# Hybrid decoder trunk: the first layer's x, AV and CV columns packed per k tile, zero matmuls during the first loads, two load queues, and the rstd spread moved

## The chip, the core and the metric

The kernel runs on one core of a Trainium2 chip. The metric is the device time of one execution in microseconds (us), lower is better; a kernel's time is the median of several executions. TensorE (PE) multiplies, ScalarE (ACT) and VectorE (DVE) do the elementwise work, GpSimd (POOL) a little scalar work, and the sync engine (SP) issues nearly all loads.

## What is computed

Two layers over x of 256 rows (t) by 1024 columns; each projects one RMS-normalised x to 3584 columns, feeds three branches, gates them and adds an output projection to x. Cut to what matters here:

```python
hn = rms_norm(x, norm_gain)
proj = jnp.einsum('bsd,de->bse', hn, w_in)
a_q, a_k, a_v, a_g, b_x, b_g, c_q, c_k, c_v, c_g = jnp.split(proj, _in_split_points(), axis=-1)
y_a = dilated_attention(rope(a_q), rope(a_k), a_v) * jax.nn.silu(a_g)      # 8 heads of 64
y_b = rg_lru_branch(b_x, ...) * jax.nn.silu(b_g)
y_c = stick_breaking_attention(c_q, c_k, c_v) * jax.nn.silu(c_g)           # 4 heads of 64
x = x + jnp.einsum('bse,ed->bsd', jnp.concatenate([y_a, y_b, y_c], axis=-1), w_out)
```

All of it is float32. After the second layer a last rms_norm follows.

## The kernel before

**Split products.** Every projection is made of three float32r products: an operand is split into a high part (a rounded copy by ScalarE, L106 or L114) and a low part (the difference, by VectorE, L107 or L115), and hi*hi, hi*lo and lo*hi are summed in PSUM (`mm3`, L166 to L172). `xh`, `xl` hold x transposed, as eight k tiles of 128 by 256; `whi`, `wlo` a chunk of weights.

**Chunks.** The weights of a layer are 18 chunks of 128 by 2048 (1 MB): AV in two chunks (four k tiles of 512 columns each), CV, CQ, CK and the others (eight k tiles of 256 columns). `load_chunk` (L95) loads a chunk into two staging tiles `st` (five buffers) and splits it in pieces of 512 columns; `whi` and `wlo` have four buffers each. `weights(l, c)` (L120) has the chunks up to two ahead of c loaded and split. The tile framework puts the instructions of ScalarE, VectorE and the queues into an order of its own; TensorE's order is the program's.

**The start.** The first layer doesn't normalise x ahead of the projections: x is multiplied by the gain alone (`first_x`, L110, the gain is a 257th column of the x tile), and 1/rms (`rstd`) is multiplied into the projections' outputs. All loads are on SP: eight pairs of an x tile (128.5 KB) and a k tile of AV (256 KB) in turn, then CV, x itself (`xres`), constants, the small parameters `prm_t` and CQ. TensorE does AV per k tile for both t halves (L259 to L264, 48 matmuls of 512 columns), then CV (48 of 256).

**The rstd spread.** `rstd0` is computed by `rms_stats` from `xres` (L276). V of both branches gets it as a per-row scale (L286 to L289). The transposed outputs (q, k and so on) need it along the free axis: L278 to L282 put it on a diagonal, multiply that with ones on TensorE (`rb_ps`, two matmuls) and copy the result to `rb`. `scaled` (L291) multiplies an output with `rb`; `rp0` is the rope table times `rb` (L472).

**Next.** CQ and CK give qc and kc; the projection of AQ[0] follows, and between its two halves `sb_scores` (L333) multiplies kc with qc. `proj_b(c, mid)` makes a projection in two halves of 24 matmuls and calls `mid` between them.

Of the kernel before, what the change touches and what calls it, by code (L numbers as in the profile page):

```python
# [9 lines left out]
F32 = mybir.dt.float32  # L10
F32R = mybir.dt.float32r
# [4 lines left out]
P = 128  # L16
S = 256
# [26 lines left out]


@with_exitstack
def trunk_kernel(ctx: ExitStack, tc: tile.TileContext, x, xt, wpack, prm_d, gatew, gains, consts, rope, out):
    nc = tc.nc
    act, dve, pe, gps = nc.scalar, nc.vector, nc.tensor, nc.gpsimd

# [35 lines left out]
        return a.rearrange("p (b t) -> p b t", b=n)  # L86

    LN_EXP, SIGM = "natural_log_exp_and_others", "sigmoid_and_others"
    table(LN_EXP)
    ctx.enter_context(tc.manual_schedule(engines={mybir.EngineType.PE}))  # L90

    xh = sb.tile([P, NK, S], F32R, name="xh", tag="xh")
    xl = sb.tile([P, NK, S], F32R, name="xl", tag="xl")

    def load_chunk(l, c, parts=2, between=None):  # L95
        hi = wsp.tile([P, 2048], F32R, name="whi", tag="whi")
        lo = wsp.tile([P, 2048], F32R, name="wlo", tag="wlo")
        w = 2048 // parts
        for i in range(parts):
            if between:  # L100
                between(i)
            st = wst.tile([P, 1024], F32, name="st", tag="st")
            nc.sync.dma_start(out=st[:, 0:w], in_=wpack[l, c][:, i * w:(i + 1) * w])
            for j in range(0, w, 512):
                ws, ss = slice(i * w + j, i * w + j + 512), slice(j, j + 512)
                act.activation(hi[:, ws], st[:, ss], AF.Copy)  # L106
                dve.tensor_sub(lo[:, ws], st[:, ss], hi[:, ws].bitcast(F32))  # L107
        return hi, lo

    def first_x(k):  # L110
        xg = scr(S + 1)
        nc.sync.dma_start(out=xg, in_=xt[k])
        g = xg[:, S:S + 1]
        act.activation(xh[:, k, :], xg[:, 0:S], AF.Copy, scale=g)  # L114
        dve.scalar_tensor_tensor(xl[:, k, :], xg[:, 0:S], g, xh[:, k, :].bitcast(F32), ALU.mult, ALU.subtract)  # L115

    order = [(l, c) for l in range(L) for c in range(NCH)]
    ready = {}
    pending = list(order)

# [4 lines left out]
            ready[i] = load_chunk(*i)  # L125
        return ready.pop((l, c))

    for i in range(2):
        ready[pending.pop(0)] = load_chunk(0, CH_AV + i, 4, lambda j, i=i: first_x(4 * i + j))
    ready[pending.pop(0)] = load_chunk(0, CH_CV)  # L130

    xres = cst.tile([P, NT, D], F32, name="xres")
    for t in range(NT):
        nc.sync.dma_start(out=xres[:, t, :], in_=x[t * P:(t + 1) * P, :])
# [1 line left out]
    ident = con[:, C_ID:C_ID + P]  # L136
    nmask = con[:, C_NM:C_NM + 384]
    nc.sync.dma_start(out=con, in_=consts[:, 0:C_CM])
    prm_t = cst.tile([P, L, SM_P], F32, name="prm_t")
    nc.sync.dma_start(out=prm_t, in_=prm_d)  # L140
    ready[pending.pop(0)] = load_chunk(0, CH_CQ)

    tiny = cst.tile([P, 1], F32, name="tiny")
    dve.memset(tiny, 1e-19)
# [30 lines left out]
    nc8 = cst.tile([P, L * 2], F32, name="nc8")  # L175

    def log_sigmoid_lambda():
        lam = prm_t.rearrange("p l (b j) -> p (l b) j", b=2)[:, :, 7:8].rearrange("p b j -> p (b j)")

        def tn(name):  # L180
            return wk.tile([P, L * 2], F32, name=name, tag=name, bufs=1)

        lneg, labs, e, d2, sv, s2, acc, lmin = [tn(f"ls{i}") for i in range(8)]
        gps.tensor_scalar(lneg, lam, -1.0, None, ALU.mult)
        dve.tensor_tensor(labs, lam, lneg, ALU.max)
        tab(e, labs, AF.Exp, scale=-1.0)
# [18 lines left out]
    gn = cst.tile([P, D], F32, name="gn", tag="gn")  # L205

    for l in range(L):
        prm = prm_t[:, l, :].rearrange("p (b j) -> p b j", b=2)
        if l > 0:
            xh = sb.tile([P, NK, S], F32R, name="xh", tag="xh")  # L210
            xl = sb.tile([P, NK, S], F32R, name="xl", tag="xl")
# [20 lines left out]
        def rows(ps, b=2):  # L232
            return v2(ps, b), rb.rearrange("p (o t) -> p o t", o=1).broadcast_to([P, b, S])

        if l == 0:
            av_w = [weights(l, CH_AV + i, 0) for i in range(2)]
        else:
            for t in range(NT):
                rstd = rms_stats(t)
                for half in range(2):  # L240
                    xn = scr(512)
                    cs = slice(half * 512, half * 512 + 512)
                    dve.scalar_tensor_tensor(xn, xres[:, t, cs], rstd, gn[:, cs], ALU.mult, ALU.mult)
                    tp = bank(at, "s")
                    for j in range(4):
                        pe.transpose(tp[:, j * P:(j + 1) * P], xn[:, j * P:(j + 1) * P], ident)  # L246
                    ks = slice(half * 4, half * 4 + 4)
                    split_psum(tp.rearrange("p (k c) -> p k c", k=4),
                               xh[:, ks, t * P:(t + 1) * P], xl[:, ks, t * P:(t + 1) * P])
                if t == 0:  # L250
                    av_w = [weights(l, CH_AV + i) for i in range(2)]
                    av_ps = [bank(at, "s")]
                    for i in range(2):
                        proj_a(av_ps[0], av_w[i], 0, 4 * i, 4, 512, i == 0, i == 1)

        if l == 0:
            av_ps = [bank(at, "s") for _ in range(NT)]
            for i in range(2):
                for k in range(4):  # L259
                    for t in range(NT):  # L260
                        v = [a.rearrange("p (k c) -> p k c", c=512)[:, k:k + 1, :].rearrange("p k c -> p (k c)")
                             for a in av_w[i]]
                        proj_a(av_ps[t], v, t, 4 * i + k, 1, 512, i + k == 0, i + k == 4)
            cv_w = weights(l, CH_CV, 1)  # L264
        else:
# [340 lines left out]
    return wp  # L606


def _pack_small(conv_w, conv_b, gate_a_w, gate_a_b, gate_x_w, gate_x_b, lru_lambda):
    pr = np.zeros((P, L, SM_P), np.float32)  # L610
    gw = np.zeros((P, L, SM_W), np.float32)
    for l in range(L):
        for b in range(2):
            r = slice(b * P, b * P + P)
            o = 8 * b
            pr[:, l, o:o + 4] = conv_w[l][:, r].T
            pr[:, l, o + 4] = conv_b[l][r]
            pr[:, l, o + 5] = gate_a_b[l].reshape(-1)[r]
            pr[:, l, o + 6] = gate_x_b[l].reshape(-1)[r]
            pr[:, l, o + 7] = lru_lambda[l][r]  # L620
# [7 lines left out]
def _arrays(x, norm_gain, w_in, conv_w, conv_b, gate_a_w, gate_a_b, gate_x_w, gate_x_b,  # L628
# [32 lines left out]
```

## Time and profile before

| | |
|---|---|
| median of 3 runs | 258.06 us (257.77 to 258.25) |
| the profiled execution | 257.8 us, span 256.0 us |
| TensorE busy | 243.4 us, 95% of the span |
| VectorE, ScalarE busy | 191.5 us (75%), 166.2 us (65%) |
| mean granted TensorE clock | 0.994 |
| chain that ended last | PE 93%, ACT 3%, DMA 1% |
| DMA | 43.44 MB, mean 170 GB/s |

The span runs from the first to the last instruction; the execution's own time is 1.8 us longer. The busy share of an engine is an average over all stages. The chain is followed back from the last instruction, at each step to what released it. Idle time stands with what ended it.

### The profile page before, as it was taken

The page shows a single profiled execution, that of the slowest core. Times are in us where ns is not written, and L with a number is a line of the kernel's source. Part 1 is how long each engine was busy: PE and PEld are TensorE (multiplying, and loading weights), DVE is VectorE, ACT ScalarE, POOL GpSimd, SP SyncE. Part 2 cuts the span into 40 slices and gives each one's busy share as a digit, 9 for nine tenths or more (in the row PEclk, how much of TensorE's full clock was granted, in tenths as well). Part 3 has the DMA queues.
Part 4 walks back from the last instruction along what each step waited for, and adds up shares of the span by engine and source line. Part 5 has one row for each costly group of instructions (what it writes and reads, how often), then busy time and mean ns, then how long its engine had stood idle before and what let it go on. Part 6 is the DMA issues. An engine that isn't in the chain of part 4 may idle for free.

```text
span 256.0 us, 4715 instructions
## 1 busy us (share of the span) xinstructions
PE 243.4 (95%) x1764; PEld 222.7 (87%) x1764; DVE 191.5 (75%) x431; ACT 166.2 (65%) x359; POOL 8.2 (3%) x29
## 2 busy tenths in 40 slices
PE   1999999999999999999999999999999999999990
PEld 1789899999999989878877999999999998987870
DVE  3864797999999669988685634499999846985253
ACT  4859866964684875994664555594486496795143
POOL 0003800000000000000000000000000000000000
PEclk9999999999999999999999999999999999999997
DMA  6999889854336840258466667532644642000022
GB/s 167 342 353 414 308 232 332 280 188 135 113 111 223 278 159 15 67 186 263 143 195 215 209 208 226 183 87 79 177 155 121 236 139 82 3 0 0 3 82 82
DMA packets 14134, 43.44 MB, mean 170 GB/s; under 512 B 1696, under 2 KB 2848, under 8 KB 14112
## 3 DMA queue, kind: packets, MB, share of 16 engines
q1 hardware_dynamic: 14112, 43.15, 50.6%
q8 instruction: 14, 0.23, 0.4%
q14 instruction: 8, 0.07, 0.1%
HBM read 42.09 MB, written 1.05 MB: 169 GB/s over the span
## 4 chain that ended last, share of the span: by engine, by line
PE 93%; ACT 3%; DMA 1%; DVE 0%; issue 0%; SPq 0%
PE pp L172 67%; PE s L172 13%; PE y L328 3%; PE s L396 2%; PE s L418 2%; ACT whi L106 1%; PE s L369 1%; PE pp L444 1%; DMA st<-w_pack 1%; PE s L342 1%; ACT scr L154 1%; PE s L246 0%; PE s L349 0%; PE s L367 0%; PE s L345 0%; ACT vc L289 0%
## 5 line engine op out<-in xcount | busy, mean ns | idle before, releaser
L107 DVE TENSOR_TENSOR wlo<-st,whi 128x512 fp32r<-128x512 f32 x144 | 93.1, 686 | 24.0 <-ACT whi L106 22.7
L106 ACT ACTIVATE whi<-st 128x512 fp32r<-128x512 f32 x144 | 82.1, 624 | 30.8 <-PE pp L172 10.5
L172 PE MATMUL pp<-xh,whi 128*128 128x256 f32 x352 | 50.8, 286 | 0.5 <-ACT whi L106 0.5
L172 PE MATMUL pp<-xl,whi 128*128 128x256 f32 x352 | 49.4, 283 | 0.0
L172 PE MATMUL pp<-xh,wlo 128*128 128x256 f32 x352 | 49.4, 283 | 0.0
L172 PEld LDWEIGHTS pp<-xh,whi 128*128 128x128 f32 x352 | 45.9, 191 | 2.4 <-issue 1.3
L172 PEld LDWEIGHTS pp<-xh,wlo 128*128 128x128 f32 x352 | 45.4, 192 | 0.0
L172 PEld LDWEIGHTS pp<-xl,whi 128*128 128x128 f32 x352 | 45.4, 192 | 0.0
L81 ACT ACTIVATE pr<-scr,mn 128x128 f32<-128x128 f32 (+1 forms) x32 | 14.1, 441 | 9.9 <-DVE mn L404 9.9
L172 PE MATMUL s<-whi,xh 128*128 128x512 f32 x32 | 11.9, 432 | 5.6 <-ACT whi L106 5.3
L154 ACT ACTIVATE scr<-xres 128x512 f32<-128x512 f32 x12 | 7.5, 626 | 12.9 <-DVE xres L542 12.8
L172 PE MATMUL pp<-whi,yh 128*128 128x512 f32 x48 | 14.1, 394 | 0.0
L172 PE MATMUL pp<-wlo,yh 128*128 128x512 f32 x48 | 13.8, 390 | 0.0
L172 PE MATMUL pp<-whi,yl 128*128 128x512 f32 x48 | 13.8, 389 | 0.0
L316 ACT ACTIVATE yh<-scr 128x512 fp32r<-128x512 f32 x8 | 5.0, 630 | 12.7 <-DVE scr L315 12.7
L172 PEld LDWEIGHTS s<-whi,xh 128*128 128x128 f32 x32 | 6.4, 205 | 7.4 <-ACT whi L106 5.3
L75 ACT ACT_TABLE_LOAD x9 | 11.5, 1283 | 0.9 <-PEq L654 0.7
L172 PE MATMUL s<-wlo,xh 128*128 128x512 f32 x32 | 11.6, 424 | 0.0
L81 ACT ACTIVATE scr<-scr 128x384 f32<-128x384 f32 (+1 forms) x20 | 10.8, 542 | 0.8 <-DVE scr L294 0.5
L172 PE MATMUL s<-whi,xl 128*128 128x512 f32 x32 | 11.3, 413 | 0.0
L172 PEld LDWEIGHTS pp<-wlo,yh 128*128 128x128 f32 x48 | 9.0, 188 | 1.9
L172 PEld LDWEIGHTS pp<-whi,yl 128*128 128x128 f32 x48 | 9.0, 188 | 1.9
(139 smaller groups left out, 321.6 us busy)
## 6 DMA issues: line engine op xcount, KB each, us to landing
st<-w_pack SPq DMA_DIRECT2D x68, 512.0 KB, 5.0
st<-w_pack SPq DMA_DIRECT2D x8, 256.0 KB, 4.6
scr<-x_t SPq DMA_DIRECT2D x8, 128.5 KB, 4.4
xres<-x_in SPq DMA_DIRECT2D x2, 512.0 KB, 7.8
out<-scr SPq DMA_DIRECT2D x4, 256.0 KB, 2.2
gw_t<-gate_w SPq DMA_DIRECT2D x2, 256.0 KB, 6.1
gn<-gains SPq DMA_DIRECT2D x1, 512.0 KB, 7.2
gf<-gains SPq DMA_DIRECT2D x1, 512.0 KB, 4.5
```

Of the source, the lines that this page charges most:

```text
L75: load = act.preload_act_table_set(name)
L81: i = dep(act.activation(*a, **k), loaded["load"])
L106: act.activation(hi[:, ws], st[:, ss], AF.Copy)
L107: dve.tensor_sub(lo[:, ws], st[:, ss], hi[:, ws].bitcast(F32))
L154: act.activation(scr(512), xres[:, t, i * 512:(i + 1) * 512], AF.Square, accum_out=sq[:, i:i + 1])
L172: pe.matmul(ps, a(k), b(k), start=first and i == 0, stop=last and i == len(seq) - 1)
L316: act.activation(yh[:, k0:k0 + n, :], dst, AF.Copy)
L328: pe.matmul(y[hr, p * 128 + o:p * 128 + 256], vt[:, s0, hs], wts[i][:, ws], start=s0 == 0, stop=s0 == 1)
L342: pe.matmul(zs[h][:, 0:256], kc[hr, hb, 0:128], qc[hr, hb, :], start=True, stop=True)
L369: pe.matmul(z[:, 0:384], trir[:, 0, :], sv, start=False, stop=True, skip_group_check=True)
L396: pe.matmul(sps[h][:, cs], qT[h0][hr, hb, t * P:(t + 1) * P], kT[h0][hr, hb, 0:(t + 1) * P], start=True, stop=True)
L418: pe.transpose(tp[:, i * P:(i + 1) * P], prob[h0 + h][:, j * P:(j + 1) * P], ident)
```

## The change

- The host packs, for the first layer, each k tile of x (256 columns), AV (512) and CV (256) into one tile `first[k]` of 128 by 1024. The gain of the first layer moves into `prm_t` as eight more columns.
- Each tile 1 to 7 is loaded by one DMA on SP. Tile 0 comes in three: x and the CV part on SP, the AV part on ACT's queue, which also loads `prm_t`.
- Seven matmuls of a zeroed bf16 tile (`cold`) into a spare PSUM bank stand at the head of TensorE's order.
- TensorE goes through the k tiles once and does AV and CV of a tile (6 matmuls of 512 columns, 6 of 256) in it. CV takes two PSUM banks instead of one.
- Splits are made per k tile: 256 columns of x, 768 of weights (`whi` and `wlo` buffers hold two tiles). In tile 0 VectorE makes the high part of AV.
- The two spread matmuls and what precedes them (`rows_of_rstd`) are now called between the halves of CK; `scaled(qc)` and `rp0` come after that.

```diff
-    for i in range(2):
-        ready[pending.pop(0)] = load_chunk(0, CH_AV + i, 4, lambda j, i=i: first_x(4 * i + j))
-    ready[pending.pop(0)] = load_chunk(0, CH_CV)
-
+    cold = sb.tile([P, 512], BF16, name="cold", tag="th")
+    dve.memset(cold, 0.0)
+    prm_t = cst.tile([P, L * SM_P + NK], F32, name="prm_t")
+    st0 = [wst.tile([P, 1024], F32, name="st", tag="st")]
+    nc.sync.dma_start(out=st0[0][:, 0:S], in_=first[0][:, 0:S])
+    act.dma_start(out=st0[0][:, S:S + 512], in_=first[0][:, S:S + 512])
+    act.dma_start(out=prm_t, in_=prm_d)
+    nc.sync.dma_start(out=st0[0][:, S + 512:1024], in_=first[0][:, S + 512:1024])
+    table(LN_EXP)
+    av_ps = [bank(at, "s") for _ in range(NT)]
+    cv_bk = [bank(pp, "pp") for _ in range(NT)]
+    warm = bank(yp, "y")
+    for i in range(WARM):
+        pe.matmul(warm, cold[:, 0:P], cold, start=True, stop=True)
+    pair = None
+    for k in range(NK):
+        st = st0[0] if k == 0 else wst.tile([P, 1024], F32, name="st", tag="st")
+        if k > 0:
+            nc.sync.dma_start(out=st, in_=first[k])
+        g = prm_t[:, L * SM_P + k:L * SM_P + k + 1]
+        if k % 2 == 0:
+            pair = [wsp.tile([P, 2048], F32R, name=n, tag=n) for n in ("whi", "wlo")]
+        o = k % 2 * 768
+        hi, lo = [a[:, o:o + 768] for a in pair]
+        act.activation(xh[:, k, :], st[:, 0:S], AF.Copy, scale=g)
+        if k == 0:
+            dve.tensor_copy(hi[:, 0:512], st[:, S:S + 512])
+            act.activation(hi[:, 512:768], st[:, S + 512:1024], AF.Copy)
+        else:
+            act.activation(hi, st[:, S:1024], AF.Copy)
+        dve.scalar_tensor_tensor(xl[:, k, :], st[:, 0:S], g, xh[:, k, :].bitcast(F32), ALU.mult, ALU.subtract)
+        for c in ((0, 512), (512, 768)) if k == 0 else ((0, 768),):
+            dve.tensor_sub(lo[:, c[0]:c[1]], st[:, S + c[0]:S + c[1]], hi[:, c[0]:c[1]].bitcast(F32))
+        for ps, c in ((av_ps, slice(0, 512)), (cv_bk, slice(512, 768))):
+            for i, (a, b) in enumerate(((xh, hi), (xl, hi), (xh, lo))):
+                for t in range(NT):
+                    pe.matmul(ps[t][:, 0:c.stop - c.start], a[:, k, t * P:(t + 1) * P], b[:, c],
+                              start=k == 0 and i == 0, stop=k == NK - 1 and i == 2)
+
+    ready[pending.pop(0)] = load_chunk(0, CH_CQ)
...
-    prm_t = cst.tile([P, L, SM_P], F32, name="prm_t")
-    nc.sync.dma_start(out=prm_t, in_=prm_d)
-    ready[pending.pop(0)] = load_chunk(0, CH_CQ)
...
         if l == 0:
             rstd0 = [rms_stats(t) for t in range(NT)]
+
+        def rows_of_rstd():
             rb_ps = bank(yp, "y")
...
-        scaled(qc, proj_b(CH_CQ), 0.125)
+        cq_ps = proj_b(CH_CQ)
+        if l > 0:
+            scaled(qc, cq_ps, 0.125)
...
-        scaled(kc, proj_b(CH_CK))
+        ck_ps = proj_b(CH_CK, rows_of_rstd if l == 0 else None)
+        if l == 0:
+            scaled(qc, cq_ps, 0.125)
+            for i in range(2):
+                dve.tensor_mul(rp0[:, i, :], rp[:, i, :], rb)
+        scaled(kc, ck_ps)
```

**ScalarE at the start.** Before, in a row (L114 is an x tile's high part, L106 a piece of weights'):

```order
L75 ACT_TABLE_LOAD
L114 ACTIVATE xh<-scr 128x256
L106 ACTIVATE whi<-st 128x512
L114 ACTIVATE xh<-scr 128x256
L106 ACTIVATE whi<-st 128x512
```

And now (L142 is x, L145 the CV part of tile 0, L147 the weights of a later tile):

```order
L123 DMA st<-first 128x512
L124 DMA prm_t<-prm 128x40
L76 ACT_TABLE_LOAD
L145 ACTIVATE whi<-st 128x256
L142 ACTIVATE xh<-st,prm_t 128x256 x2
L147 ACTIVATE whi<-st 128x768
```

Two DMA issues stand ahead of the table load, and the first xh stands behind the split of the CV part.

**ScalarE behind the first tiles.** Before (L154 is a square with its sum, L288 and L289 are va and vc; the first row's last pieces are of CV, CQ's come behind the second va):

```order
L106 ACTIVATE whi<-st 128x512 x5
L154 ACTIVATE scr,sq<-xres 128x512 x2
...
L288 ACTIVATE va<-s,rstd 128x512
L106 ACTIVATE whi<-st 128x512 x2
L289 ACTIVATE vc<-pp,rstd 128x256 x2
L106 ACTIVATE whi<-st 128x512 x20
```

And now (L103 are pieces of weights, L177 the squares, L301 and L302 va and vc):

```order
L103 ACTIVATE whi<-st 128x512 x4
L177 ACTIVATE scr,sq<-xres 128x512 x2
...
L301 ACTIVATE va<-s,rstd 128x512
L302 ACTIVATE vc<-pp,rstd 128x256
L103 ACTIVATE whi<-st 128x512 x18
```

All four pieces of CQ now stand ahead of the squares.

**VectorE from rb to kc.** Before (L282 is rb, L472 the rope table, L294 qc and then kc):

```order
L282 COPY rb<-y 128x256
L472 TENSOR_TENSOR rp_197<-rp,rb 128x256
L107 TENSOR_TENSOR wlo<-st,whi 128x512 x2
...
L107 TENSOR_TENSOR wlo<-st,whi 128x512 x4
L294 SCALAR_TENSOR_TENSOR qc<-pp,rb 128x512
...
L107 TENSOR_TENSOR wlo<-st,whi 128x512 x4
L294 SCALAR_TENSOR_TENSOR kc<-pp,rb 128x512
```

And now (L295 is rb, L307 qc and then kc, L496 the rope table):

```order
L490 CAST trir<-scr 128x128
L295 COPY rb<-y 128x256
L307 SCALAR_TENSOR_TENSOR qc<-pp,rb 128x512
L104 TENSOR_TENSOR wlo<-st,whi 128x512 x4
L496 TENSOR_TENSOR rp_285<-rp,rb 128x256 x2
L307 SCALAR_TENSOR_TENSOR kc<-pp,rb 128x512
```

What was spread over some forty rows now stands together, behind the spread matmuls in the middle of CK.

## Rows read from the trace of the kernel before

**Rows 1.** The page's part 1: busy us, share and instructions of each engine.

```profile
PE 243.4 (95%) x1764; PEld 222.7 (87%) x1764; DVE 191.5 (75%) x431; ACT 166.2 (65%) x359; POOL 8.2 (3%) x29
```

**Rows 2.** Waits of TensorE: who waited for whom, us in total, times, longest.

```profile
PE s L172 <- ACT whi L106: 5.3, 1, 5.3
PE pp L172 <- ACT whi L106: 0.5, 1, 0.5
PE s L172 <- ACT xh L164: 0.3, 1, 0.3
```

**Rows 3.** Timeline, first loads and splits: start, us, engine, line, operation, out<-in.

```profile
0.72 0.38 SPq L112 DMA_DIRECT2D scr<-x_t  x1
...
1.16 0.42 SPq L103 DMA_DIRECT2D st<-w_pack  x1
...
2.89 0.51 ACT L114 ACTIVATE xh<-scr 128x256 fp32r<-128x256 f32 x1 [0.89 <-DMA scr<-x_t]
...
4.63 0.63 ACT L106 ACTIVATE whi<-st 128x512 fp32r<-128x512 f32 x1 [1.24 <-DMA st<-w_pack]
```

**Rows 4.** Stretches: length, busy us per engine, granted clock, DMA share, GB/s.

```profile
4.00:4.50 0.50, 0.00 (x0) 0.00 (x0) 0.00 (x0) 0.00 (x0) 0.00 (x0) 1.00 0.93 240
...
9.00:10.00 1.00, 1.00 (x3) 0.76 (x3) 1.00 (x4) 0.98 (x3) 0.00 (x0) 1.00 1.07 366
```

**Rows 5.** Timeline of TensorE, AV: first, second, two slow, twelfth and last matmul.

```profile
5.32 0.79 PE L172 MATMUL s<-whi,xh 128*128 128x512 f32 x1 [5.32 <-ACT whi L106]
...
6.04 0.80 PE L172 MATMUL s<-wlo,xh 128*128 128x512 f32 x1
...
9.19 0.63 PE L172 MATMUL s<-whi,xl 128*128 128x512 f32 x1
...
9.62 0.63 PE L172 MATMUL s<-whi,xh 128*128 128x512 f32 x1
...
10.47 0.40 PE L172 MATMUL s<-whi,xl 128*128 128x512 f32 x1
...
18.67 0.39 PE L172 MATMUL s<-whi,xl 128*128 128x512 f32 x1
```

**Rows 6.** Timeline of TensorE, CV, the rstd spread (L281) and CQ's first matmuls.

```profile
18.90 1.12 PE L172 MATMUL pp<-whi,xh 128*128 128x256 f32 x8
19.85 1.12 PE L172 MATMUL pp<-wlo,xh 128*128 128x256 f32 x8
...
24.66 0.60 PE L281 MATMUL y<-scr,ones 128*128 128x128 f32 x4
25.02 0.72 PE L172 MATMUL pp<-xh,whi 128*128 128x256 f32 x4
26.26 1.02 PE L172 MATMUL pp<-xh,whi 128*128 128x256 f32 x4 [0.53 <-ACT whi L106]
27.12 1.11 PE L172 MATMUL pp<-xl,whi 128*128 128x256 f32 x8
```

**Rows 7.** Timeline of ScalarE: CQ's first two pieces, vc, CQ's last two.

```profile
23.60 1.14 ACT L106 ACTIVATE whi<-st 128x512 fp32r<-128x512 f32 x2
...
24.85 0.84 ACT L289 ACTIVATE vc<-pp,rstd 128x256 f32<-128x256 f32 x2
...
25.58 1.15 ACT L106 ACTIVATE whi<-st 128x512 fp32r<-128x512 f32 x2
```

**Rows 8.** Timeline of VectorE from rb to kc, and TensorE's scores (L342).

```profile
25.46 0.42 DVE L282 COPY rb<-y 128x256 f32<-128x256 f32 x1
...
32.11 0.69 DVE L294 SCALAR_TENSOR_TENSOR qc<-pp,rb 128x512 f32<-128x512 f32 x1 [1.22 <-PE pp L172]
...
35.40 2.50 DVE L107 TENSOR_TENSOR wlo<-st,whi 128x512 fp32r<-128x512 f32 x4
37.88 0.69 DVE L294 SCALAR_TENSOR_TENSOR kc<-pp,rb 128x512 f32<-128x512 f32 x1
...
40.64 0.70 PE L342 MATMUL s<-qc,kc 64*128 64x256 f32 x4
```

**Rows 9.** DMA issues: out<-in, issuer, count, KB each, us to landing.

```profile
prm_t<-prm SPq DMA_DIRECT2D x1, 16.0 KB, 7.9
```

More of the change, by code (lines that the diff above doesn't have):

```diff
@@ L31 @@
 SCR = 7
+WARM = 7
 C_ID = 0
@@ L46, in trunk_kernel @@
 @with_exitstack
-def trunk_kernel(ctx: ExitStack, tc: tile.TileContext, x, xt, wpack, prm_d, gatew, gains, consts, rope, out):
+def trunk_kernel(ctx: ExitStack, tc: tile.TileContext, x, first, wpack, prm_d, gatew, gains, consts, rope, out):
     nc = tc.nc
@@ L88, in trunk_kernel @@
     LN_EXP, SIGM = "natural_log_exp_and_others", "sigmoid_and_others"
-    table(LN_EXP)
     ctx.enter_context(tc.manual_schedule(engines={mybir.EngineType.PE}))
@@ L93, in trunk_kernel, with load_chunk @@
     xl = sb.tile([P, NK, S], F32R, name="xl", tag="xl")
-    def load_chunk(l, c, parts=2, between=None):
+    def load_chunk(l, c):
         hi = wsp.tile([P, 2048], F32R, name="whi", tag="whi")
         lo = wsp.tile([P, 2048], F32R, name="wlo", tag="wlo")
[L98 to L101, printed above, removed]
+        for i in range(2):
             st = wst.tile([P, 1024], F32, name="st", tag="st")
-            nc.sync.dma_start(out=st[:, 0:w], in_=wpack[l, c][:, i * w:(i + 1) * w])
-            for j in range(0, w, 512):
-                ws, ss = slice(i * w + j, i * w + j + 512), slice(j, j + 512)
+            nc.sync.dma_start(out=st, in_=wpack[l, c][:, i * 1024:(i + 1) * 1024])
+            for j in range(0, 1024, 512):
+                ws, ss = slice(i * 1024 + j, i * 1024 + j + 512), slice(j, j + 512)
                 act.activation(hi[:, ws], st[:, ss], AF.Copy)
@@ L108, in load_chunk @@
         return hi, lo
[L110 to L117, printed above, removed]
+    order = [(l, c) for l in range(L) for c in range(NCH) if l > 0 or c > CH_CV]
     ready = {}
@@ L177, in log_sigmoid_lambda @@
     def log_sigmoid_lambda():
-        lam = prm_t.rearrange("p l (b j) -> p (l b) j", b=2)[:, :, 7:8].rearrange("p b j -> p (b j)")
+        lam = prm_t[:, 0:L * SM_P].rearrange("p (q j) -> p q j", q=2 * L)[:, :, 7:8].rearrange("p b j -> p (b j)")
         def tn(name):
@@ L207, in trunk_kernel @@
     for l in range(L):
-        prm = prm_t[:, l, :].rearrange("p (b j) -> p b j", b=2)
+        prm = prm_t[:, l * SM_P:(l + 1) * SM_P].rearrange("p (b j) -> p b j", b=2)
         if l > 0:
@@ L233, in rows @@
             return v2(ps, b), rb.rearrange("p (o t) -> p o t", o=1).broadcast_to([P, b, S])
-        if l == 0:
-            av_w = [weights(l, CH_AV + i, 0) for i in range(2)]
-        else:
+        if l > 0:
             for t in range(NT):
@@ L254, in trunk_kernel @@
                         proj_a(av_ps[0], av_w[i], 0, 4 * i, 4, 512, i == 0, i == 1)
[L256 to L265, printed above, removed]
             cv_w = weights(l, CH_CV)
-        cv_ps = bank(pp, "pp")
-        if l > 0:
+            cv_ps = bank(pp, "pp")
             av_ps.append(bank(at, "s"))
@@ L271, in trunk_kernel @@
                 proj_a(av_ps[1], av_w[i], 1, 4 * i, 4, 512, i == 0, i == 1)
-        for t in range(NT):
-            proj_a(cv_ps[:, t * 256:(t + 1) * 256], cv_w, t, 0, 8, 256, True, True)
+            for t in range(NT):
+                proj_a(cv_ps[:, t * 256:(t + 1) * 256], cv_w, t, 0, 8, 256, True, True)
+            cv_bk = [cv_ps[:, t * 256:(t + 1) * 256] for t in range(NT)]
         if l == 0:
             rstd0 = [rms_stats(t) for t in range(NT)]
+        def rows_of_rstd():
             rb_ps = bank(yp, "y")
@@ L288, in trunk_kernel @@
             act.activation(va[:, t, :], av_ps[t], AF.Copy, scale=sc)
-            act.activation(vc[:, t, :], cv_ps[:, t * 256:(t + 1) * 256], AF.Copy, scale=sc)
+            act.activation(vc[:, t, :], cv_bk[t][:, 0:256], AF.Copy, scale=sc)
         def scaled(dst, ps, sc=1.0):
@@ L467, in trunk_kernel @@
             log_sigmoid_lambda()
-        scaled(qc, proj_b(CH_CQ), 0.125)
+        cq_ps = proj_b(CH_CQ)
+        if l > 0:
+            scaled(qc, cq_ps, 0.125)
         if l == 0:
-            for i in range(2):
-                dve.tensor_mul(rp0[:, i, :], rp[:, i, :], rb)
             tri = scr(2 * P)
@@ L478, in trunk_kernel @@
             dve.tensor_scalar(trir[:, 1, :], ones, -1.0, None, ALU.mult)
-        scaled(kc, proj_b(CH_CK))
+        ck_ps = proj_b(CH_CK, rows_of_rstd if l == 0 else None)
+        if l == 0:
+            scaled(qc, cq_ps, 0.125)
+            for i in range(2):
+                dve.tensor_mul(rp0[:, i, :], rp[:, i, :], rb)
+        scaled(kc, ck_ps)
         rotate(proj_b(CH_AQ[0], sb_scores), qT, 0, "q0")
@@ L606, in _pack_weights, with _pack_small @@
     return wp
-def _pack_small(conv_w, conv_b, gate_a_w, gate_a_b, gate_x_w, gate_x_b, lru_lambda):
-    pr = np.zeros((P, L, SM_P), np.float32)
+def _pack_small(norm_gain, conv_w, conv_b, gate_a_w, gate_a_b, gate_x_w, gate_x_b, lru_lambda):
+    pr = np.zeros((P, L * SM_P + NK), np.float32)
+    pr[:, L * SM_P:] = norm_gain[0].reshape(NK, P).T
     gw = np.zeros((P, L, SM_W), np.float32)
@@ L614, in _pack_small @@
             r = slice(b * P, b * P + P)
[L615 to L620, printed above, removed]
+            o = l * SM_P + 8 * b
+            pr[:, o:o + 4] = conv_w[l][:, r].T
+            pr[:, o + 4] = conv_b[l][r]
+            pr[:, o + 5] = gate_a_b[l].reshape(-1)[r]
+            pr[:, o + 6] = gate_x_b[l].reshape(-1)[r]
+            pr[:, o + 7] = lru_lambda[l][r]
             for g, w in enumerate((gate_a_w, gate_x_w)):
@@ L633, in _arrays @@
     x2 = x.reshape(S, D)
-    pr, gw = _pack_small(conv_w, conv_b, gate_a_w, gate_a_b, gate_x_w, gate_x_b, lru_lambda)
+    pr, gw = _pack_small(norm_gain, conv_w, conv_b, gate_a_w, gate_a_b, gate_x_w, gate_x_b, lru_lambda)
     return {
         "x_in": np.ascontiguousarray(x2),
-        "x_t": np.concatenate([x2.T.reshape(NK, P, S), norm_gain[0].reshape(NK, P, 1)], 2),
+        "first": np.concatenate([x2.T.reshape(NK, P, S), w_in[0].reshape(NK, P, 3584)[:, :, 1024:1536],
+                                 w_in[0].reshape(NK, P, 3584)[:, :, 3072:3328]], 2),
         "w_pack": _pack_weights(w_in, w_out),
```

## The prediction

> **What bounds the kernel now.** I read the busy shares first: TensorE is busy for 95% of the span [rows 1], so only idle or slow stretches of TensorE can give time back, or a new stall take it. Its waits come next: in 256 us it waits three times, 5.3 us for its first operands, 0.5 us for weights of chunk CQ and 0.3 us at the layer border [rows 2]. The change touches the first two. The timeline then shows a third loss that no wait names. The 48 matmuls of AV start at 5.32 us and the 12th at 10.47 us, while the other 36 steps, to the start at 18.67, take 0.228 us each [rows 5]: the first twelve take 5.15 us where 11 steps at the later pace would be 2.5. [...] The granted clock does not show the step, it is recorded as 1.00 before and behind it [rows 4], so I take the level from the pace. What came before the rise was five microseconds of matmuls with one pause of some 0.3 us (a first matmul at 0.43, the next start 0.72 later).
>
> So up to the scores of the stick-breaking branch TensorE loses 5.32 us of waiting, 2.65 us of low clock and pause, and 1.14 us at CQ, whose first eight matmuls take 25.02 to 27.12 where eight take 0.96 elsewhere (18.90 to 19.85) [rows 6]. That last one is ScalarE's: it splits the last two pieces of CQ only at 25.58, behind the statistics, va and vc [rows 7]. Sum of the losses: 9.1 us.
>
> **The sum is made** against the profiled execution, 257.8 us for a span of 256.0 us; it stands 0.26 us under the median of 258.06, and I carry the difference over.
>
> **When the first real matmul starts.** It needs the high part of x (the split of 256 columns, with the gain from prm_t) and whi. By the order, ScalarE does the 256 CV columns first and then xh, so two loads decide: the third piece of tile 0 (second on SP) and prm_t (second on ACT's queue). Ahead of both, or with them, lie 128 + 256 + 128 + 20 = 532 KB. Before, 128.5 + 256 KB, issued at 0.72 and 1.16, had landed at 4.63 [rows 3]. The extra 148 KB take 0.6 us at the 240 GB/s of that moment [rows 4]; issuing from two engines at once saves the 0.44 us between the two issues. That gives 4.8 us. Behind it ScalarE has two operations of about 0.5 us (a 128x256 split took 0.51 [rows 3]), the first of which I take as mostly hidden because its piece can land a little sooner: 5.4 us. Bounds: 4.3 us if the third piece lands as fast as the first x tile did (2.17 us after its issue at 1.16) and both splits follow; 5.8 us if nothing is hidden. I keep 5.4, nearest to the row that moved a like amount. So the two queues bring nothing at this place: 5.32 becomes 5.4.
>
> [...] No run so far shows two queues.
>
> **The zero matmuls.** Seven of 512 columns at 0.43 us are 3.0 us. The engines are free at 0.7 us, a fill on VectorE precedes; I take 1.1 to 4.1 us. They lie wholly inside the wait and cost nothing unless they are still running when data is there (bound: 4.3, so no). If they count as the AV matmuls did, the rise comes 5.15 us after the first, near 6.3 us, provided the pause from 4.1 to 5.4 us is not held against them. Neither zero operands nor a pause of 1.3 us is in the trace: bounds are a rise at 5.4 or before (no slow real matmul) and a rise 5.15 us after the first real one, 10.5 us.
>
> [...]
>
> **AV and CV per tile.** The work is the same: 48 matmuls of 512 columns and 48 of 256, only in another order. A tile is 6 x 0.228 + 6 x 0.12 = 2.09 us at the high level (0.12 is an eighth of 0.96 [rows 6]), eight tiles 16.7 us. Tile 0 from 5.4 us, low until 6.3, is done at 7.9. Tile 1 is 512 KB behind the 532: 1.4 us at 366 GB/s, 2.1 at 240 [rows 4]; I take 1.7, landed at 6.5; then xh 0.5 and 768 columns of whi at 0.9 (1.5 x 0.63 [rows 3], less a little overhead): ready at 7.9 too. I count 8.0. This is the floor for an earlier clock: TensorE would wait here instead. From tile 2 on a tile asks 1.4 us of ScalarE, about as much of VectorE (0.5 for xl, 0.9 for wlo) and 1.4 us of the DMA queues, against 2.09 us of TensorE; five staging buffers and four pairs of split buffers let them run ahead. The constants of the recurrence, which prm_t's early arrival lets in among the tiles, cost ScalarE one operation and VectorE three small ones, inside that spare time. End of CV: 8.0 + 7 x 2.09 = 22.6 us, where before it was 24.66: **-2.1 us**.
>
> **CQ.** Its four splits now stand ahead of the statistics on ScalarE: tile 7 lands near 6.5 + 6 x 1.4 = 15 us, its splits end at 16.4, CQ's own at about 19, against the need at 22.6. The stall of 1.14 us goes: **-1.1 us**. Cover: 3.6 us; it is gone only if the loads stay at the 240 GB/s of the start [rows 4] throughout. Late next would be CK: ScalarE reaches it after va and vc, 22.6 + about 1.5 us, and TensorE needs it at 22.6 + 6 x 0.96 = 28.4.
>
> **The rstd spread.** The two matmuls (0.36 us, 24.66 to 25.02 [rows 6]) move from before CQ into the middle of CK: 0. But now rb, qc, four wlo pieces, both rp products and kc stand in one row on VectorE behind them. From the start of CQ: the spread is issued at 9 x 0.96 = 8.64; rb starts 0.80 later (24.66 to 25.46), then 0.45, qc 0.61, four pieces 2.48 (35.40 to 37.88), rp 2 x 0.42 by the copy of that size, kc 0.69 [rows 8]: kc is there at 14.5. The scores need it at 15 x 0.96 + 0.36 = 14.8. It just fits, by a quarter of a microsecond; before, kc had 2.1 us (38.57 against 40.64). I take 0; bounds 0 and 1.0 (the four pieces waiting for ScalarE).
>
> **Other loads.** The sixteen small loads of x and AV become eight of 512 KB, and the bytes are the same; prm_t no longer stands between consts and CQ. SP is moved past nothing that TensorE waits for. 0.
>
> **Sum:** 5.4 for 5.32 us, the clock and tile 1 together -2.1, CQ -1.1, the spread 0: -3.2 us. 257.8 - 3.2 = 254.6 in the profiled run, 258.06 - 3.2 = **254.9 us** in the median.
>
> **Rivals.**
> - *The clock rises no sooner* (zeros don't count, or the pause undoes them). For it: nothing in the trace tells either way, and the pause is four times the one that the trace shows. Against it: a pause of 0.3 us did not hold the rise up. Then CV ends at 5.4 + 16.7 + 2.6 = 24.7, as before, and only CQ's 1.1 us is left: 256.9 us. Chance 0.22.
> - *kc becomes a wait.* The margin of 0.25 us fails where one of the four pieces is late or VectorE waits for ScalarE; about 0.7 us in the middle, 255.6 us. For it: the four pieces stand between rb and kc. Against it: their weights should be split long before. Chance 0.12.
> - *prm_t late, the time goes up.* Every xh now waits for prm_t, 128 rows of 160 bytes on ACT's queue beside full rows on SP's. Before, this load took 7.9 us to land [rows 9], queued behind some 2 MB. If it did so again, from 1.15 us, xh would be ready at 9.6, the pause would cost the clock, and CV would end at 9.6 + 16.7 + 2.6 = 28.9: 3.1 us later than the 25.8 us (24.66 + 1.14) that now count, 261.1 us. It decides from a landing at 6.0 us on. Against it: only 256 KB stand ahead of it on its queue. Chance 0.06.
> - *The change does not bring its loads forward* is no rival but in the sum already: 5.4 for 5.32.
>
> **How the numbers follow.** The forecast has 0.60; its own range goes from 253.6 (first matmul at 4.3, tile 1 ready at 6.7 instead of 8.0, that is 1.3 better) to 255.6 (first matmul at 5.8, tile 1 at 8.5). The first rival's 256.9 has to be inside to leave no more than 2 in 10 out: 253.6 to 257.1. About 0.2%, half a microsecond, is what a measurement of this kernel can tell from no change: faster 0.92, same 0.03, slower 0.05.
>
> **What would show it.** Seven matmuls on cold from about 1.1 to 4.1 us; the first real one near 5.4 us; a pace of 0.228 us for 512 columns by tile 1, at 8 us; CV done near 22.6; no wait in CQ; kc done before the scores' first matmul; from there on every piece of TensorE's timeline some 3.2 us earlier. A pace of 0.43 us beyond 9 us would be the first rival, a wait before the scores the second, a first xh after 6.5 us, released by prm_t, the third. The forecast is wrong altogether if TensorE stalls later in layer 0 because weights, now asked for 3 us earlier, come no sooner.

## The result, and the profile after

The changed kernel takes 256.15 us (median of 4 runs, 255.86 to 256.68) beside 258.12 us for the kernel before: ratio 0.9928, with a 95% interval of 0.9909 to 0.9948. Measured again later it was 256.11 us, ratio 0.9920 (0.9896 to 0.9944). So it is 2.0 us faster where 3.2 us were forecast. The profiled execution took 255.86 us for a span of 254.1 us.

The page's part 1 for the changed kernel answers to [rows 1], and TensorE's waits (who waited for whom, us in total, times, longest) to [rows 2]:

```profile
PE 244.1 (96%) x1771; PEld 221.7 (87%) x1771; DVE 191.4 (75%) x430; ACT 165.0 (65%) x355; POOL 11.2 (4%) x29
```

```profile
PE y L131 <- DVE cold L119: 1.2, 1, 1.2
PE s L154 <- ACT whi L147: 1.1, 1, 1.1
PE s L154 <- DVE wlo L150: 0.9, 1, 0.9
PE s L195 <- ACT xh L187: 0.3, 1, 0.3
```

CQ's 0.5 us of waiting is gone. The 5.3 us for the first operands are now filled with zero matmuls but for 1.2 us ahead of them (for the fill) and 0.9 us behind them. A new wait has come, 1.1 us for the weights of tile 1. The timeline shows it (start, us, engine, line, operation); it answers to [rows 3] and [rows 5]:

```profile
1.17 3.17 PE L131 MATMUL y<-cold 128*128 128x512 bf16 x7 [1.17 <-DVE cold L119]
...
4.71 0.49 ACT L142 ACTIVATE xh<-st,prm_t 128x256 fp32r<-128x256 f32 x1
...
5.26 0.73 PE L154 MATMUL s<-whi,xh 128*128 128x512 f32 x2 [0.93 <-DVE wlo L150]
...
5.83 0.67 PE L154 MATMUL s<-whi,xl 128*128 128x512 f32 x2
...
6.34 0.63 PE L154 MATMUL s<-wlo,xh 128*128 128x512 f32 x2
...
7.43 0.51 ACT L142 ACTIVATE xh<-st,prm_t 128x256 fp32r<-128x256 f32 x1 [2.23 <-DMA st<-first]
7.85 0.83 ACT L147 ACTIVATE whi<-st 128x768 fp32r<-128x768 f32 x1
...
8.73 0.74 PE L154 MATMUL s<-whi,xh 128*128 128x512 f32 x2 [1.05 <-ACT whi L147]
```

The first real matmul starts at 5.26 us, and from there a pair of 512 columns takes 0.47 to 0.57 us, 0.23 to 0.29 for one. That is the fast pace, which the kernel before has at 0.228 us from 10.47 us on, some five microseconds later; its slow pace is 0.43 us (9.19 to 9.62 in [rows 5]). The recorded texts call the two the high and the low level. In the kernel without the zeros (below) the rise from the slow pace to the fast one comes at 10.3 us; with them it comes this early in some executions only. Tile 0 is done near 7.5 us, tile 1 lands only at 7.4, and its splits last until 8.7. The end of this stretch answers to [rows 6]; it is again TensorE's timeline:

```profile
23.49 0.40 PE L154 MATMUL pp<-wlo,xh 128*128 128x256 f32 x2
23.73 1.13 PE L195 MATMUL pp<-xh,whi 128*128 128x256 f32 x8
24.69 1.12 PE L195 MATMUL pp<-xl,whi 128*128 128x256 f32 x8
...
32.37 0.61 PE L294 MATMUL y<-scr,ones 128*128 128x128 f32 x4
...
38.66 0.70 PE L355 MATMUL s<-qc,kc 64*128 64x256 f32 x4
```

CV ends at 23.73 (before 24.66), and CQ's first eight matmuls take 0.96 us (before 2.10). The scores start at 38.66 where they started at 40.64: 1.98 us earlier, and the span is 1.9 us shorter, so all of the change lies ahead of the scores. VectorE's and ScalarE's rows show what CQ and kc owe that to, beside [rows 7] and [rows 8]:

```profile
18.52 2.35 ACT L103 ACTIVATE whi<-st 128x512 fp32r<-128x512 f32 x4 [1.94 <-DMA st<-w_pack]
...
26.37 5.01 ACT L103 ACTIVATE whi<-st 128x512 fp32r<-128x512 f32 x8
```

```profile
33.01 0.42 DVE L295 COPY rb<-y 128x256 f32<-128x256 f32 x1 [0.32 <-PE y L294]
...
37.15 0.68 DVE L307 SCALAR_TENSOR_TENSOR kc<-pp,rb 128x512 f32<-128x512 f32 x1
```

CQ's four pieces are split from 18.5 to 20.9, three microseconds ahead of need. CK's first piece, at 26.37 behind vc, is ready at 27.0, 2.5 us ahead of 29.5, and kc 0.8 us ahead of the scores.

One thing comes later than before. The diff puts CQ's load (1 MB) ahead of x itself, and its splits ahead of the statistics. ScalarE's first square, before and after, starts when the first half of x lands:

```profile
19.00 0.63 ACT L154 ACTIVATE scr<-xres 128x512 f32<-128x512 f32 x1 [0.17 <-DMA xres<-x_in]
```

```profile
21.09 0.63 ACT L177 ACTIVATE scr<-xres 128x512 f32<-128x512 f32 x1 [0.21 <-DMA xres<-x_in]
```

x lands 2.1 us later, 0.2 us behind the end of CQ's splits, and with it come the statistics, both rstd, va, vc and the splits of CK behind them.

### The profile page after: what moved, and what is told of

The parts are those of the page before. It is cut to its first block, busy times and chain, and to the rows that moved or that the text cites. A ratio compares the mean times of both kernels' runs of the same rounds, so it can differ in the third digit from the quotient of the medians.

```text
span 254.1 us, 4707 instructions
## 1 busy us (share of the span) xinstructions
PE 244.1 (96%) x1771; PEld 221.7 (87%) x1771; DVE 191.4 (75%) x430; ACT 165.0 (65%) x355; POOL 11.2 (4%) x29
## 4 chain that ended last, share of the span: by engine, by line
PE 92%; ACT 3%; DMA 2%; SPq 0%; DVE 0%; issue 0%
PE pp L195 65%; PE s L195 8%; PE s L154 4%; PE y L341 3%; PE s L409 2%; DMA st<-first 2%; PE s L431 2%; PE pp L154 2%; PE s L382 1%; PE pp L457 1%; ACT whi L103 1%; PE s L355 1%; ACT scr L177 1%; PE s L267 0%; PE s L362 0%; PE s L380 0%
## 5 line engine op out<-in xcount | busy, mean ns | idle before, releaser
L104 DVE TENSOR_TENSOR wlo<-st,whi 128x512 fp32r<-128x512 f32 x132 | 84.8, 685 | 21.1 <-ACT whi L103 19.9
L103 ACT ACTIVATE whi<-st 128x512 fp32r<-128x512 f32 x132 | 74.9, 623 | 25.3 <-PE pp L195 10.8
L177 ACT ACTIVATE scr<-xres 128x512 f32<-128x512 f32 x12 | 7.5, 626 | 13.2 <-DVE xres L560 13.0
L417 DVE CUSTOM_DVE_ANT_0 scr<-s,con 128x128 f32<-128x128 f32 (+1 forms) x32 | 10.2, 349 | 0.0
L195 PEld LDWEIGHTS pp<-whi,yh 128*128 128x128 f32 x48 | 8.7, 188 | 1.6
L422 DVE TENSOR_SCALAR pr<-pr,den 128x128 f32<-128x128 f32 (+1 forms) x32 | 8.7, 314 | 0.0
L560 DVE TENSOR_TENSOR xres<-pp,xres 128x512 f32<-128x512 f32 x6 | 4.1, 689 | 5.4 <-PE pp L195 5.3
```

The source lines that it names most:

```text
L177: act.activation(scr(512), xres[:, t, i * 512:(i + 1) * 512], AF.Square, accum_out=sq[:, i:i + 1])
L195: pe.matmul(ps, a(k), b(k), start=first and i == 0, stop=last and i == len(seq) - 1)
L417: dve.tensor_tensor_reduce(xs[:, cs], sps[h][:, cs], nmask[:, cs], -0.125, 3e38, ALU.add, ALU.min, mn[:, t:t + 1])
L422: dve.tensor_scalar(pr[:, cs], pr[:, cs], den[:, t:t + 1], None, ALU.mult)
```

## The experiments

Every kernel was timed over five rounds beside the kernel before on the same chip; medians are given with the ratio to it and its interval.

**Taking one part of the change away.** First the zeros:

```diff
-WARM = 7
+WARM = 0
```

> The changed kernel without its seven zero matmuls. Theory (the zeros raise the clock before the first real matmul): tile 0 runs at 0.43 us per 512 columns from 5.3 us, the pace rises only near 10.4 us, CV ends near 24.8 instead of 23.73, so +1.1 us, about 257.2 us. Rival (tile 1's late landing at 7.4 us hides whatever the zeros save): tile 0 is slow but done when tile 1 is there at 8.7 and little is lost, +0.0 to +0.4 us, 256.2 to 256.5 us.

256.62 us, 0.9947 (0.9927 to 0.9966). The median is half a microsecond above the changed kernel's, between the theory's 1.1 and the rival's 0.0 to 0.4, but the intervals overlap, so the worth of the zeros is not clear of noise. In the profile the slow pace reaches to 10.3 us, as the theory had it, and TensorE's timeline has CQ start, at CV's end, here:

```profile
24.62 1.12 PE L195 MATMUL pp<-xh,whi 128*128 128x256 f32 x8
25.59 1.12 PE L195 MATMUL pp<-xl,whi 128*128 128x256 f32 x8
```

CV ends when it ended before (24.66), CQ's first eight matmuls take 0.97 us, and by the changed kernel's 14.93 us from CQ to the scores these start at some 39.55, an estimate, 1.09 us earlier than before; the span, 255.0 us, is 1.0 us shorter. So what stands without the zeros, 1.5 us in the median, is in this execution CQ's stall alone, and the packed loads had not brought CV's end forward.

Then the spread, called before CQ again:

```diff
+        if l == 0:
+            rows_of_rstd()
         cq_ps = proj_b(CH_CQ)
...
-        ck_ps = proj_b(CH_CK, rows_of_rstd if l == 0 else None)
+        ck_ps = proj_b(CH_CK)
```

> The changed kernel with the rstd spread back before CQ. Theory (the move became necessary once CV ends earlier): the second rstd was ready at 25.3 us while CV ends at 23.73, so TensorE waits some 2 us there and the time is about 258.2 us. Rival (as the prediction put it, the move is worth nothing): 256.2 us.

257.47 us, 0.9991 (0.9968 to 1.0015): 1.3 us lost, not told apart from the kernel before. The theory had it at some 2 us. TensorE's timeline of that kernel shows where:

```profile
23.99 0.38 PE L294 MATMUL y<-scr,ones 128*128 128x128 f32 x2
25.31 0.49 PE L294 MATMUL y<-scr,ones 128*128 128x128 f32 x2 [0.94 <-DVE scr L293]
25.55 1.20 PE L195 MATMUL pp<-xh,whi 128*128 128x256 f32 x8
```

ScalarE makes the second rstd in the kernel before and in this one at

```profile
22.78 0.20 ACT L81 ACTIVATE rstd<-lnv 128x1 f32<-128x1 f32 x1
```

```profile
24.74 0.19 ACT L82 ACTIVATE rstd<-lnv 128x1 f32<-128x1 f32 x1
```

It is ready at 24.9 us here, 0.9 us behind CV's end (23.99). Before, it was ready at 23.0, 1.7 us ahead of CV's end (24.66), and the spread cost no wait. So 1.7 us of room became 0.9 us of waiting: 0.7 us of that is CV's earlier end, and 2.0 us are the later statistics, which CQ's load and splits now precede. The rival falls.

Then the second queue:

```diff
-    act.dma_start(out=st0[0][:, S:S + 512], in_=first[0][:, S:S + 512])
-    act.dma_start(out=prm_t, in_=prm_d)
+    nc.sync.dma_start(out=st0[0][:, S:S + 512], in_=first[0][:, S:S + 512])
+    nc.sync.dma_start(out=prm_t, in_=prm_d)
```

> The changed kernel with all first loads on SP, in the order x, AV part, prm_t, CV part of tile 0, then tiles 1 to 7. Theory (the queue saves issue time only, and tile 1 sets the pace anyway): the first real matmul 0.0 to 0.5 us later, tile 1 as before within 0.5 us, 256.0 to 256.6 us. Rival (the second queue brings the loads forward): first matmul and tile 1 later by 1 us or more, 257.2 us or more.

255.88 us, 0.9916 (0.9896 to 0.9937): no loss. ScalarE's timeline of it:

```profile
5.25 0.51 ACT L142 ACTIVATE xh<-st,prm_t 128x256 fp32r<-128x256 f32 x1 [3.25 <-DMA prm_t<-prm]
...
6.87 0.51 ACT L142 ACTIVATE xh<-st,prm_t 128x256 fp32r<-128x256 f32 x1 [0.81 <-DMA st<-first]
```

The first xh starts half a microsecond later than in the changed kernel's profile (4.71; 4.7 to 5.2 in ten executions with two queues), and nothing comes of it: tile 1 lands at 6.9, TensorE goes from tile 0 to tile 1 at 8.16, and CV ends at 23.03.

**Adding a part to the kernel before.** The zeros alone (the same seven matmuls ahead of its AV):

> The kernel before with the seven zero matmuls alone. Theory (the clock's gain is kept only together with CQ's earlier split): AV runs at the high level from about 6 us and CV ends some 2 us earlier, near 22.7 us, but CQ's last pieces are still split at about 25.6 us, behind vc, so TensorE waits there and the time falls by 0.0 to 0.4 us only, 257.7 to 258.1 us. Rival (the zeros are the whole gain): 256.0 to 256.2 us.

258.10 us, 0.9998 (0.9985 to 1.0012): nothing. TensorE's waits and timeline of that kernel:

```profile
PE pp L178 <- ACT whi L107: 2.1, 2, 1.3
```

```profile
6.35 0.40 PE L178 MATMUL s<-whi,xh 128*128 128x512 f32 x1
6.58 0.40 PE L178 MATMUL s<-wlo,xh 128*128 128x512 f32 x1
...
25.42 0.95 PE L178 MATMUL pp<-xh,whi 128*128 128x256 f32 x4
27.11 1.02 PE L178 MATMUL pp<-xh,whi 128*128 128x256 f32 x4 [0.74 <-ACT whi L107]
```

AV does run at 0.23 us per 512 columns from 6 us on; then TensorE waits 1.3 us in CV and 0.7 us in CQ for weights, and CV ends at 25.06, not near 22.7 as the theory had it. The slow pace of before (0.43 us, up to 10.47 us) had hidden how little ahead the weights were. The second half of CV landed at 17.7 us before and was needed at 19.4; here it is needed at 17.9 and lands at 18.7 (at 18.0 in the next kernel).

Zeros and moved spread together, loads and splits as before:

> The kernel before with the zero matmuls and with the rstd spread moved into CK, all loads and splits as before. Theory (without the packed tiles and CQ's earlier split, TensorE waits for CV's and CQ's weights whatever the clock): 0.0 to 0.5 us less than before, 257.6 to 258.1 us. Rival (zeros and spread make the change, the packing is worth nothing): 256.0 to 256.4 us.

258.15 us, 1.0001 (0.9984 to 1.0018): nothing either. In its profile the waits for CV's weights (1.0 us) and CQ's (0.17 and 0.74 us) stand. So neither zeros nor spread pays without the new start, and the new start pays 1.5 us without the zeros. No run has the packed loads without CQ's earlier splits, or the other way round; that the 1.5 us are CQ's is read from the profile of the kernel without zeros alone.

**What the forecast's missing microsecond waits for.** Ten zeros, so that no pause is left behind them:

```diff
-WARM = 7
+WARM = 10
```

> The changed kernel with ten zero matmuls instead of seven, 1.2 to about 5.4 us, so that no pause is left before the first real matmul. Theory (the pause is what lets tile 0 run at the low level in some executions): tile 0 is at the high level in every execution, tile 1's landing alone decides, about 0.3 to 0.6 us less, 255.5 to 255.9 us. Rival (the pause plays no part): same as with seven within 0.2 us, 256.0 to 256.3 us; were the zeros an obstacle to tile 0, some tenths more.

256.02 us, 0.9904 (0.9878 to 0.9931), not told apart from seven zeros. Its profiled execution is the instructive one. TensorE's timeline:

```profile
5.60 0.73 PE L154 MATMUL s<-whi,xh 128*128 128x512 f32 x2
...
22.57 1.12 PE L195 MATMUL pp<-xh,whi 128*128 128x256 f32 x8
...
28.33 1.94 PE L195 MATMUL pp<-xh,whi 128*128 128x256 f32 x8
30.10 1.11 PE L195 MATMUL pp<-xl,whi 128*128 128x256 f32 x8
...
38.54 0.70 PE L355 MATMUL s<-qc,kc 64*128 64x256 f32 x4 [0.18 <-DVE kc L307]
```

and ScalarE's:

```profile
23.91 0.63 ACT L177 ACTIVATE scr<-xres 128x512 f32<-128x512 f32 x1 [0.72 <-DMA xres<-x_in]
...
27.52 4.65 ACT L103 ACTIVATE whi<-st 128x512 fp32r<-128x512 f32 x8
```

Here everything that the forecast asked for came true: the fast pace from the start (a pair of 512 columns in 0.46 to 0.57 us), tile 1 landed at 6.1, CV done at 22.57 (forecast 22.6). And the span is 254.1 us, no shorter than with CV done at 23.73. The microsecond is lost again at CK, whose first eight matmuls take 1.77 us (28.33 to 30.10) instead of 0.96, and 0.18 us at kc: CK's splits stand behind the statistics, and those wait for the second half of x to land (23.9 us; the changed kernel's profile has no wait there). So in this execution the loads set the time.

Tile 1 split as tile 0 is (VectorE casts the AV part, ScalarE 256 columns):

```diff
-        if k == 0:
+        if k < 2:
             dve.tensor_copy(hi[:, 0:512], st[:, S:S + 512])
...
-        for c in ((0, 512), (512, 768)) if k == 0 else ((0, 768),):
+        for c in ((0, 512), (512, 768)) if k < 2 else ((0, 768),):
```

> The changed kernel with tile 1 split as tile 0: VectorE makes the high part of its AV columns while ScalarE makes xh, then ScalarE only 256 columns. Theory (TensorE waits for tile 1's splits, 1.3 us behind its landing at 7.4): in executions with tile 0 at the high level tile 1 starts 0.5 to 0.75 us sooner; where tile 0 is slow nothing changes; median 0.2 to 0.6 us less, 255.5 to 255.9 us. Rival (VectorE's extra cast and two pieces delay later tiles): 256.2 us or more.

256.28 us, 0.9924 (0.9900 to 0.9947): no gain. In its profiled execution TensorE ran at the slow pace up to 9.1 us (a pair of 512 columns in 0.85 to 1.02 us), so tile 1's splits were not the limit there, and the theory's case, tile 0 at the high level, was not seen. Both edits:

> Both of the two edits: ten zero matmuls, and tile 1 split as tile 0. Theory (two limits in series, the clock and tile 1's splits, so that together they bring more than either): 0.7 to 1.2 us less than the changed kernel, 255.0 to 255.4 us. Rival (one of them hides the other): no better than the better of the two alone.

255.41 us, 0.9892 (0.9865 to 0.9918); the median is 0.6 us under the better of the two, but the intervals overlap. Its profiled execution (255.88 us) doesn't show the theory's way: the fast pace came at 6.4 us (a pair of 512 columns in 1.02 us ahead of it, 0.54 behind), tile 1 landed at 7.8, and CV ended at 23.77.

The changed kernel again, for the comparison and for a second look at its start:

> The changed kernel once more, on the chip of the runs below. Every theory: 255.9 to 256.4 us. The start varies between executions: either tile 0 is at the high level and tile 1's landing decides, or tile 0 is at the low level up to about 9 us; CV ends between 22.6 and 24.0 us.

256.11 us. This time TensorE's timeline began so:

```profile
5.48 1.22 PE L154 MATMUL s<-whi,xh 128*128 128x512 f32 x2 [1.14 <-ACT xh L142]
6.50 1.05 PE L154 MATMUL s<-whi,xl 128*128 128x512 f32 x2
...
23.98 1.12 PE L195 MATMUL pp<-xh,whi 128*128 128x256 f32 x8
```

A pair of 512 columns takes 0.85 to 1.02 us, 0.43 to 0.51 for one: the slow pace, in spite of the zeros. Tile 1 had landed at 6.7, and it was tile 0 that was late. CV ends within 0.25 us of the other execution, by the other way.

Last, CK ahead of x itself and the statistics, to take away the wait that ten zeros had met:

```diff
-    ready[pending.pop(0)] = load_chunk(0, CH_CQ)
+    for c in (CH_CQ, CH_CK):
+        ready[pending.pop(0)] = load_chunk(0, c)
```

> The changed kernel with CK loaded and split right behind CQ, ahead of x itself and the statistics. Theory (the loads in order of need are the bound: an earlier CV end is lost again at CK, whose splits stand behind the statistics): in executions where CV ends at 23.7 or later CK did not wait and nothing is gained; 0.0 to 0.4 us less than the changed kernel, 255.7 to 256.2 us. Rival (statistics 2.5 us later hold up rb, kc or the PSUM banks of va and vc): 256.4 us or more.

257.02 us, 0.9951 (0.9928 to 0.9974): the median is 0.9 us above the changed kernel's, as the rival had it, but the intervals overlap (0.9896 to 0.9944). In its profile x lands at 24.7, behind another 1 MB, the rest of the chain is late, and the scores wait:

```profile
PE s L356 <- DVE kc L308: 0.5, 1, 0.5
```

> CK ahead of the statistics and ten zero matmuls. Theory (with ten zeros CV ended at 22.6 and 1.0 us was lost at CK, 0.2 at kc): the wait at CK goes, the time falls by 0.6 to 1.0 us against ten zeros alone (256.0), to 255.0 to 255.4 us. Rival (later waits, at kc or at the weights of AQ, take all of it back because the loads are the bound at every later chunk too): 255.8 to 256.1 us.

255.82 us, 0.9910 (0.9888 to 0.9931). CK's weights are there, and now its PSUM bank is not, because vc is copied out of it later:

```profile
PE pp L196 <- ACT vc L303: 0.7, 1, 0.7
```

0.2 us under ten zeros alone and not told apart from it, by the median the rival's outcome: the wait has moved to the next that hangs on x. With tile 1's splits as well:

> Ten zero matmuls, tile 1 split as tile 0, and CK ahead of the statistics. Theory (three limits in series): 254.6 to 255.2 us. Rival (the loads are the bound behind them): 255.4 us, as without CK's move, or more.

255.04 us (254.84 to 255.19, 4 runs), 0.9883 (0.9865 to 0.9901): faster than both kernels, by about 1.1 us than the changed one (the intervals just touch, 0.9896 to 0.9944 there), and not told apart from the same kernel without CK's move (255.41 us). In its profile neither CQ nor CK nor kc waits; TensorE goes from 22.73 (CQ) to 28.49 (CK) and on to the scores without a stop:

```profile
22.73 1.12 PE L196 MATMUL pp<-xh,whi 128*128 128x256 f32 x8
...
28.49 1.12 PE L196 MATMUL pp<-xh,whi 128*128 128x256 f32 x8
...
37.66 0.70 PE L356 MATMUL s<-qc,kc 64*128 64x256 f32 x4
```

The scores start 2.98 us earlier than in the kernel before (40.64), close to the 3.2 us that were forecast. x landed at 23.1 us in that execution, at 25.0 with ten zeros and CK moved. Whether splitting tile 1 earlier, which frees staging buffers sooner, brought that about, or whether it was that execution's luck, the runs don't show.

## Why the prediction was right, and where it was not

The direction and the range (253.6 to 257.1) held, and of the mechanism CQ's term; the term of the clock and tile 1 came at less than half. The forecast of 254.9 was 1.25 us too low. The range held although the larger term did not: it had been drawn wide enough for the first rival's 256.9. (Its own upper end, 255.6, is 0.2 us more than a tile 1 ready at 8.5 instead of 8.0 gives.)

- **First real matmul at 5.4 us:** 5.26, and 5.3 to 5.8 in nine more executions with two queues. Two queues brought nothing at this place, as said, and one queue did as well: 255.88 us with one, 256.11 with two.
- **prm_t late:** did not happen; xh started at 4.71.
- **The clock, with tile 1, -2.1 us:** this is the step that failed, on size; -0.93 us was measured (24.66 to 23.73; -0.68 in the second look). It put the rise "near 6.3 us" and tile 1 at 8.0. That the rise comes 5.15 us behind the first zero was an estimate, and so were two levels of the clock, taken from the pace. What the runs show is a pace of 0.43 or 0.23 us per 512 columns, beside a granted clock of 1.00 in both kernels' profiles, and a rise at various times behind the first zero (1.17 us): 4.1 us at most in the changed kernel's profile, 7.9 in the second look, 5.2 with ten zeros and tile 1's edit. What it depends on, no run shows. In the profiled execution the rise had come by 5.3, tile 1 landed at 7.4 instead of 6.5, and TensorE waited for it until 8.73; the seven tiles behind took 15.0 us instead of 14.6. In the second look tile 1 landed at 6.7 and the rise came only near 9. Both limits have to be met at once for CV to end at 22.6; both vary between executions with seven zeros, and the runs don't show with what.
- **And behind it the cover was missing:** two executions in which CV did end at 22.5 to 22.6 won next to nothing (scores at 38.54 with ten zeros, 38.43 with CK moved as well, 38.66 in the changed kernel), because CK then waited. The prediction named CK as late next and gave it 4 us of room (22.6 + 1.5 against 28.4). That sum was wrong: it had va and vc follow CV's end, but they follow the statistics. Under "Other loads" it put SP's new order at 0; but that order has CQ's 1 MB ahead of x, and the statistics start at 21.09 instead of 19.00. With CK's splits ahead as well and nothing waiting, an end of CV at 22.73 did bring the scores to 37.66.
- **CQ, -1.1 us:** right; the scores start 14.93 us after CQ does, where 15.98 us lay between CV's end and the scores before.
- **The spread, 0:** right as a sum, but the reason it is there was missed. The move costs nothing and saves 1.3 us, since the second rstd, now 2 us later, would have come behind the earlier end of CV.
- **kc just fits:** it did, by 0.8 us, and became a wait of 0.2 to 0.5 us in kernels that ran earlier or loaded x later.
- **First rival (the clock rises no sooner):** true in some executions and false in others. Over the eight profiled executions with seven zeros the first real matmul ran at the fast pace (0.23 to 0.34 us per 512 columns) in four and at the slow one (0.43 to 0.51) in four; of the six of the changed kernel and its variants, at the fast pace in two only. Where it was slow, the rise still came about a microsecond earlier than without zeros (8.9 to 9.6 us, against 10.3 to 10.5). The rival's time, 256.9 us, is within the interval of the kernel without zeros (256.62).

## What to carry to other kernels

A slow stretch at the start may be hiding that the loads are just as late: speeding it up alone (zeros in the kernel before, 258.10 us) buys nothing, so look up, for each chunk that comes after, when its data lands and what its splits stand behind, before counting the gain. When an engine's stage ends earlier, everything that used to be ready just in time has to be moved with it, as the rstd spread here (1.3 us). When a load or a split is put ahead of another, count what hangs on the one that now comes later: here x, and with it the statistics, 2 us. And a term that hangs on two events, each of which varies between executions, should be counted at the later of the two, not at the middle of each.

## What the runs showed of the hardware

- **The pace behind zeros.** In all twelve profiled executions with zeros the fast pace came by 9.6 us, in the two without at 10.3 and 10.5. In four with seven zeros the first real matmuls, from 5.0 to 5.8 us on, took 0.23 to 0.34 us per 512 columns. In four others, with the same seven zeros (1.17 to about 4.3 us), they took 0.43 to 0.51 and the rise came between 8.9 and 9.6 us. The pauses between the last zero and the first real matmul were 0.7, 0.8, 0.9 and 1.5 us in the first four, and 1.0 to 1.15 us in the others: shorter pauses went with the fast pace, but the one of 1.5 us stands against a simple rule. With ten zeros the pace was fast at once in three of four, behind pauses of 0.1, 0.2 and 0.6 us, and from 6.4 us in the fourth, which had none. In the one with 0.6 us (CK moved) the rise came among the zeros themselves: ten took 3.74 us, as shown below, where they took 4.33 to 4.45 in the other three and seven take 3.17. In the changed kernel it had come by 5.3 us in one execution and came near 9.0 in another. The granted clock in the profiles' stretches read 1.00 on both sides of the rise (in the kernel before in 9 to 10 us, as in [rows 4], and in 11 to 12 us) and showed none of it.

```profile
1.17 3.74 PE L131 MATMUL y<-cold 128*128 128x512 bf16 x10 [1.17 <-DVE cold L119]
```

- **A load of 512 KB, issued at the same moment (1.62 us in the changed kernel's profile and with ten zeros), landed between 6.0 and 7.9 us** in ten profiled executions of the same first loads (median 6.4). The bytes moved by then would have sufficed: in the changed kernel's profile the DMA engines had moved 1.5 MB by 7.0 us, tile 1 with all that was issued ahead of it is 1.07 MB, and it had not landed. Tiles 2 to 4 were issued behind it without a wait (2.1 to 3.0 us); that their bytes moved meanwhile and held it up is an estimate from these figures and was not tried. The stretches of that time (length, busy us per engine, granted clock, DMA share, GB/s):

```profile
4.00:4.50 0.50, 0.34 (x1) 0.00 (x0) 0.43 (x1) 0.11 (x1) 0.00 (x0) 1.00 0.86 198
...
6.50:7.00 0.50, 0.50 (x5) 0.41 (x4) 0.00 (x0) 0.00 (x0) 0.00 (x0) 1.00 1.04 426
```
